# Sharing the first norm's rows between two engines and ending the last row block in two column halves

## The chip, the cores and the metric

The kernel runs on one core of a Trainium2 chip. A core has five engines, each with its own instruction queue: TensorE (PE, matrix products; its weight loads are listed as PEld), VectorE (DVE, elementwise and sums), ScalarE (ACT, functions of one operand), GpSimd (POOL) and SyncE (SP, which issues transfers). They wait for one another through semaphores. The metric is the time of one execution in microseconds (us). A lower time is better.

## The reference

One layer of a decoder on 1024 tokens of width 1024: a gated linear recurrence with 8 heads of 128, then a squared-ReLU MLP of width 4096, each behind an RMS norm, and a last RMS norm.

```python
def _rmsnorm(x, gain):
    xf = x.astype(jnp.float32)
    y = xf * lax.rsqrt(jnp.mean(xf * xf, axis=-1, keepdims=True) + NORM_EPS)
    return (y * gain.astype(jnp.float32)).astype(x.dtype)

def _hgrn2_mixer(h, w_in, lower_bound, out_norm, w_out):
    proj = h @ w_in
    q, f, i, g = jnp.split(proj, 4, axis=-1)
    ...
    o = _hgrn2_chunk_scan(heads(qf), heads(k), heads(i), heads(log_f))
    ...
    return o @ w_out

def _squared_relu_mlp(h, w1, w2):
    a = jax.nn.relu(h @ w1)
    return (a * a) @ w2

# DEPTH = 1
    x = x + _hgrn2_mixer(_rmsnorm(x, norm_mix), ...)
    x = x + _squared_relu_mlp(_rmsnorm(x, norm_mlp), mlp_w1, mlp_w2)
    return _rmsnorm(x, norm_final)
```

All inputs are float32.

## The kernel before

**Precision.** Each operand of a large product is split into a high part (`hi`, rounded by ACT) and the rest (`lo`, a subtraction on DVE). `split_mm` adds three matmuls: high by high, high by low, low by high (lines 212, 213, 214). The large products work on 2 by 2 blocks with sums and differences of blocks (names `s1` to `s4`, `t1` to `t4`), which saves one product in eight. `ht` is the split of such a sum of the normed input; `R` holds the unsplit values.

**The front.** `x` is loaded in eight row blocks of 128 tokens, `xs[0]` to `xs[7]`. For row blocks 0 to 3 a loop does, per block: the row's sum of squares on ACT (`stats_1`, line 293), the addition of EPS on DVE (line 297), the power -0.5 on POOL (line 298), the scaling of the whole block on DVE (`norm_scale`, line 186), four 128x128 transposes on PE (line 195) into four PSUM banks `first_banks`, and some transposes of `ident` that keep PE busy (`keep_warm`, line 123; `WARM_ROW` has their number per block). Then `transposes_1` moves each bank into the split operand `h0B` (ACT line 325, DVE line 326), with the gain.

**The hooks.** `plain_pair` computes the projections of head 0 with whole blocks: `w0` (a, c, b, d: q and f) and `w1` (i and g), first for the tokens of row blocks 0 to 3 (half 0), then for 4 to 7. Before each step of one weight block by one operand block (three matmuls) it calls `hook()`, which takes the next piece of work from a list: the remaining transposes of half 0, `value_1` (a copy of a bank to `R`), the sums of squares of row blocks 4 to 7, one addition and one power for the four of them (`rstd_second`), their scaling, then the transposes of half 1, one list entry in two. `ensure` splits the weights ahead of their use.

**The order on the engines.** PE's order is that of the code throughout. ACT, DVE and POOL follow the code in the very first part; from the end of half 0 until late in the output projection a scheduler orders them, and after that the code again. So a change of the code in the front also moves some instructions of the scan of head 0 (`lv` on PE, `q`, `qe`, `k`, `f` and `Ac` on DVE).

**The end.** In the last product of the MLP, job `d`, the four row blocks `pb` are done one after the other: 24 matmuls of 512 columns into the bank `m2X`, then `evac_2` adds the bank to `acc` (DVE, line 1071), and `rows_second_half` does the last norm: sum of squares of columns 512 to 1023 (ACT, line 1090), addition to the sum of the first half and power (POOL, lines 1092 and 1093), scaling (ACT line 1095, DVE line 1097) and two stores. Weights and operands of these products are float32 in the form `F32R`.

Of the kernel before, what the change touches and what calls it, by code (L numbers as in the profile page):

```python
# [42 lines left out]
LAST_SPACING = 1800.0  # L43
AHEAD = 6
WARM = 36
WARM_ROW = (6, 6, 6, 4)


@with_exitstack
def trunk(ctx: ExitStack, tc: tile.TileContext, x, gains, masks, gfin, w_in, w_out, w1, w2, out):  # L50
# [131 lines left out]
    def norm_scale(hn, src, r, on_act=False):  # L182
        if on_act:
            nc.scalar.activation(hn, src, AF.Copy, scale=r[:, 0:1])
        else:
            nc.vector.tensor_scalar(hn, src, r[:, 0:1], None, op0=ALU.mult)
# [65 lines left out]
    with tc.tile_pool(name="scan", bufs=1) as sp:  # L252
# [34 lines left out]
        def stats_1(tb):  # L287

            ss = ss4[:, tb - 4:tb - 3] if tb >= 4 else pool.tile([P, 1], F32, name=f"ss{tb}", tag="ss", bufs=8)
            if tb in (5, 7):  # L290
                nc.vector.tensor_tensor_reduce(junk[1], xs[tb], xs[tb], 1.0 / D, 0.0, ALU.mult, ALU.add, ss)
            else:
                nc.scalar.activation(junk[0], xs[tb], AF.Square, scale=D ** -0.5, accum_out=ss)
            return ss

        def rstd_1(r, ss):
            nc.vector.tensor_scalar(r, ss, EPS, None, op0=ALU.add)
            nc.gpsimd.tensor_tensor(r, r, neghalf[:, :r.shape[1]], ALU.pow)

        first_banks = [transpose_bank(0, 0, kb) for kb in range(4)]  # L300
        for tb in range(4):
            rs[tb] = pool.tile([P, 1], F32, name=f"rs{tb}", tag="rs1", bufs=8)
            rstd_1(rs[tb], stats_1(tb))
            norm_scale(xs[tb], xs[tb], rs[tb])
            for kb in range(4):
                transpose_rows(first_banks[kb], xs, kb, (tb,))
            keep_warm(WARM_ROW[tb])
# [43 lines left out]
        def pieces(f, *args):  # L351
            return lambda: [f(a) for a in args]

        def scale_1(tb):
            norm_scale(xs[tb], xs[tb], rs[tb])

        first = [lambda: (one[3](), value_1(0)), lambda: value_1(1), lambda: (one[4](), value_1(2)),
                 lambda: (one[5](), value_1(3)), one[6], one[7]]
        hooks += first

        def rstd_second():
            rstd_1(rs4, ss4)
            for i in range(4):
                rs[4 + i] = rs4[:, i:i + 1]

        hooks += [pieces(stats_1, 4, 5), pieces(stats_1, 6, 7), lambda: None, rstd_second, pieces(scale_1, 4, 5),
                  pieces(scale_1, 6, 7)] + [lambda: None] * 7
        for f in transposes_1(1):
            hooks += [f, lambda: None]

# [66 lines left out]
        def plain_pair(h, tl, j, half):  # L437

            steps = [(r, k) for r in range(2) for k in range(2)]
            if j == 0:  # L440
                steps.sort(key=lambda rk: rk[1])
            bank = {}
            for r, k in steps:
                if k == 0:
                    bank[r] = psum.tile([P, 512], F32, name=f"pp{h}{j}{half}{r}", tag="d")
                p_ = bank[r]
                m = "abcd"[2 * r + k]
                w = weight(2 * h + j, m)
                for kb in range(4):
                    hook()  # L450
                    t = hc[BLOCKS[half][k], kb]
                    c = slice(kb * P, (kb + 1) * P)
                    split_mm(p_, w[:, 0, c], w[:, 1, c], t[:, 0], t[:, 1], (k, kb) == (0, 0), (k, kb) == (1, 3))
                    i = index[2 * h + j, m]
                    if (j, half, m) == (0, 0, "a"):
                        ensure(2 + kb // 2)
                    elif kb == (0 if (j, half) == (0, 0) and m in "bc" else 2):
                        ensure(min(i + 3, 4 * PLAIN) if half == 0 else i + 4)
                    pump(650.0)
                if k == 0:  # L460
                    continue
                if (j, r) == (0, 0):
                    q_part(h, tl, 512 * half, p_)
                elif j == 0:
                    f_half(h, tl, half, p_, 1.0)
                    f_bound(h, tl["f"][:, HALF[half]])
                elif r == 0:
                    tiles(h, tl, "vT")
                    nc.scalar.activation(tl["vT"][:, HALF[half]], p_, AF.Copy)
                else:  # L470
                    g_half(h, tl, half, p_, 1.0)
# [590 lines left out]
    def fs(name):  # L1062
        return pool.tile([P, 1], F32, name=name, tag="fs", bufs=14)
# [16 lines left out]
    def rows_first_half(tb):  # L1080
# [4 lines left out]
        nc.vector.tensor_tensor(acc[tb][:, :512], acc[tb][:, :512], gf[:, :512], ALU.mult)  # L1085
        small[tb] = ss

    def rows_second_half(tb):
        ot, ss = out_tile(tb), fs(f"ft{tb}")
        nc.scalar.activation(ot[:, 512:], acc[tb][:, 512:], AF.Square, scale=D ** -0.5, accum_out=ss)  # L1090
        r = fs(f"fr{tb}")
        nc.gpsimd.tensor_tensor(r, ss, small[tb], ALU.add)
        nc.gpsimd.tensor_tensor(r, r, neghalf[:, :1], ALU.pow)
        rows = slice(tb * P, (tb + 1) * P)
        nc.scalar.activation(ot[:, :512], acc[tb][:, :512], AF.Copy, scale=r[:, 0:1])
        nc.scalar.dma_start(out[rows, :512], ot[:, :512])
        nc.vector.scalar_tensor_tensor(ot[:, 512:], acc[tb][:, 512:], r[:, 0:1], gf[:, 512:],
                                       op0=ALU.mult, op1=ALU.mult)
        nc.sync.dma_start(out[rows, 512:], ot[:, 512:])

    def product_2(k, pb, s, first, last_):
        hi, lo = sides[k]
        w = ws[k]
        for p in range(2):
            o, t = slice(512 * p, 512 * p + 512), slice(P * pb, P * pb + P)
            split_mm(banks[s, 0][pb], hi[:, p, t], lo[:, p, t], w[0][:, o], w[1][:, o], first and p == 0,
                     last_ and p == 1, skip_group_check=True)

    banks = {}
# [36 lines left out]
    for k, (which, u, v, s, m, n) in enumerate(steps):  # L1146
        first = m in ("a", "s1", "b")
        ending = which == 2 and u >= 4
        if first and v == 0:
            banks[s, u if which == 1 else 0] = [psum.tile([P, 512], F32, name=f"m{which}{s}{u}{p}", tag=BANK[s]) for p in range(2 * which)]  # L1150
        load_act(k + LOOK + 2)
        if which == 1:
            w = ws.pop(k)
            for p in range(2):
                for kb in range(4):
                    o = slice((4 * p + kb) * P, (4 * p + kb + 1) * P)
                    t = hc[n, kb]
                    if k == 1 or (k, p) == (0, 1) and kb > 1:
                        hook()
                    split_mm(banks[s, u][p], w[0][:, o], w[1][:, o], t[:, 0], t[:, 1], first and kb == 0, kb == 3,  # L1160
                             skip_group_check=True)
            if u + 1 < NU and m in ("s2", "s4"):
                load_w1(u + 1, "db" if m == "s4" else "ac" if u else "c")
            if u + 1 == NU and m in ("s2", "s4", "b"):
                for x in range(4):
                    load_w2({"s2": "a", "s4": "c", "b": "d"}[m], x)
            if k <= 8:
                for f in behind_0.get(k, ()):
                    f()
                continue  # L1170
            prep(k + LOOK)
            evac_1(u, m, e[u], banks[s, u])
            continue
        if (u, m) == (4, "a"):
            gf = dp.tile([P, D], F32, name="gf", tag="d8")
            nc.sync.dma_start(gf, bass.AP(tensor=gfin.tensor, offset=gfin.offset, ap=[[0, P], [1, D]]))
        if m == "a" and u < 4:
            load_acc(u)
        if m == "s1" and u < 4:
            load_w2("b", u)  # L1180
            load_acc(u + 4)
        if ending and m == "d":
            if v == 0:
                for pb in range(4):
                    for x in range(4):
                        product_2(k + x, pb, s, False, x == 3)
                    evac_2(m, pb, banks[s, 0][pb])
                    rows_second_half(pb)
            continue
        for pb in range(4):  # L1190
            product_2(k, pb, s, first and v == 0, v == 3)
        prep(k + LOOK)
        if m == "a":
            first_sums(raw2, u, slot(4 + v, [P, D], f"vs3{u}"))
        if ending and m == "b" and v == 3:
            prep(k + 3)
        if v == 3:
            for pb in range(4):
                evac_2(m, pb, banks[s, 0][pb])
        if ending and m == "b" and v < 2:  # L1200
            rows_out(4 + 2 * v)
            rows_out(5 + 2 * v)
        if ending and m == "b" and v == 3:
            prep(k + 4)
            for pb in range(4):
                rows_first_half(pb)
# [41 lines left out]
```

## Time and profile before

| what | value |
|---|---|
| median of 3 runs | 1148.96 us (1148.83 to 1149.08) |
| the profiled execution | 1148.8 us |
| span of its instructions | 1147.0 us |
| PE / DVE / ACT / POOL busy | 1133.5 / 797.2 / 583.7 / 37.9 us |
| first matmul of the projections | 13.26 us after the span's start |
| transposes of row blocks 4 to 7 begin / the next matmul | 29.31 / 31.38 us |
| last matmul starts / end of the span | 1139.79 / 1147.0 us |
| granted TensorE clock, mean | 0.999 |

The span runs from the first to the last instruction of the profiled execution; its own time holds 1.8 us more. A row of the timeline gives the start, the duration, the engine, the line, the operation, what it writes and reads, the size, and in brackets the idle time of the engine ahead of it and what ended it. Rows of one line that follow each other directly are merged (x4). A row of a single line's view gives the durations as least/median/most in ns.

### The profile page before, as it was taken

What the parts mean: (1) busy time and instruction counts of PE and PEld (TensorE: products, weight loads), DVE (VectorE), ACT (ScalarE), POOL (GpSimd) and SP (SyncE); (2) the same over time, 40 slices, a digit from 0 to 9 for tenths busy, and PEclk for the clock granted to TensorE, in tenths of its full rate; (3) what the DMA queues carried; (4) which work ended last, traced back from release to release, by engine and by line L of the source; (5) the groups of instructions that cost most, each with busy time, mean ns of one, the idle gap of its engine ahead of it and who ended that gap; (6) DMA issues with size and microseconds to landing.
All of it is one profiled execution on the core that took longest, in us unless ns stands there. A gap on an engine that the chain in (4) does not pass through costs nothing.

```text
span 1147.0 us, 17503 instructions
## 1 busy us (share of the span) xinstructions
PE 1133.5 (99%) x7082; PEld 936.8 (82%) x7082; DVE 797.2 (70%) x1145; ACT 583.7 (51%) x1014; POOL 37.9 (3%) x67
## 2 busy tenths in 40 slices
PE   9999999999999999999999999999999999999997
PEld 7778888787878788888888888888888888888886
DVE  6997878769687785446866654565488756677673
ACT  7656556374655573247654544454452443323552
POOL 1000000000000000010000000000000000000011
PEclk9999999999999999999999999999999999999999
DMA  6112211111111273021254524452797535322331
GB/s 262 37 38 68 61 40 56 56 38 57 56 50 63 68 264 130 26 85 74 76 200 184 187 86 149 183 197 82 269 367 295 195 136 207 124 92 94 127 129 73
DMA packets 42849, 142.84 MB, mean 125 GB/s; under 512 B 4880, under 2 KB 5008, under 8 KB 42768
## 3 DMA queue, kind: packets, MB, share of 16 engines
q1 hardware_dynamic: 41904, 140.53, 34.4%
q8 instruction: 55, 0.90, 0.3%
q10 hardware_dynamic: 864, 1.20, 0.3%
q14 instruction: 26, 0.21, 0.1%
HBM read 100.55 MB, written 41.16 MB: 124 GB/s over the span
## 4 chain that ended last, share of the span: by engine, by line
PE 86%; DVE 10%; ACT 1%; issue 1%; DMA 1%; POOL 0%; POOLq 0%; DVEq 0%; ACTq 0%
PE m2X L214 5%; PE m1X L213 5%; PE m2X L212 5%; PE m1X L212 5%; PE m1X L214 5%; PE m2X L213 5%; PE pX L212 3%; PE pX L214 3%; PE pX L213 3%; PE m1Y L212 3%; PE m1Y L213 3%; PE m2Y L214 3%; PE m2Y L212 3%; PE m1Y L214 3%; PE m2Y L213 3%; PE op L212 2%
## 5 line engine op out<-in xcount | busy, mean ns | idle before, releaser
L903 ACT ACTIVATE a<-ai 128x1024 fp32r<-128x1024 f32 x56 | 59.1, 1055 | 72.1 <-PE m2X L213 24.9
L904 DVE TENSOR_TENSOR a<-ai,a 128x1024 fp32r<-128x1024 f32 x56 | 68.3, 1220 | 11.5 <-ACT a L903 11.5
L994 ACT ACTIVATE e<-e 128x1024 f32<-128x1024 f32 x24 | 25.5, 1062 | 72.5 <-DVE e L1041 72.5
L212 PE MATMUL op<-wo,zh 128*128 128x512 f32 x128 | 51.1, 399 | 0.0
L214 PE MATMUL op<-wo,zh 128*128 128x512 f32 x128 | 50.0, 391 | 0.0
L213 PE MATMUL op<-wo,zh 128*128 128x512 f32 x128 | 49.9, 390 | 0.0
L1071 DVE TENSOR_TENSOR acc<-acc,m2X 128x512 f32<-128x512 f32 x32 | 21.1, 685 | 35.7 <-PE m2X L214 35.6
L145 DVE TENSOR_TENSOR xr<-xr,op 128x512 f32<-128x512 f32 x24 | 16.4, 687 | 38.1 <-PE op L214 38.1
L379 DVE TENSOR_TENSOR q<-q,f 128x512 f32<-128x512 f32 x56 | 38.5, 687 | 2.1 <-PE lv L627 2.1
L386 DVE TENSOR_TENSOR k<-k,f 128x512 f32<-128x512 f32 x56 | 38.3, 684 | 0.0
L991 ACT ACTIVATE e<-e 128x1024 f32<-128x1024 f32 x32 | 34.0, 1062 | 1.0
L604 ACT ACTIVATE AT<-Ac 32x256 f32<-32x256 f32 x32 | 13.3, 415 | 36.4 <-DVE Ac L600 36.1
L145 DVE TENSOR_TENSOR raw<-raw,raw 128x512 f32<-128x512 f32 x42 | 28.9, 688 | 0.8
L214 PEld LDWEIGHTS op<-wo,zh 128*128 128x128 f32 x128 | 24.0, 188 | 5.2
L212 PEld LDWEIGHTS op<-wo,zh 128*128 128x128 f32 x128 | 24.0, 188 | 4.8
L213 PEld LDWEIGHTS op<-wo,zh 128*128 128x128 f32 x128 | 24.1, 188 | 4.7
L696 ACT ACTIVATE z<-o,rs_z 128x128 f32<-128x128 f32 x64 | 17.4, 384 | 16.4 <-POOL rs_z L115 16.4
L1022 ACT ACTIVATE e<-m1X 128x512 f32<-128x512 f32 x30 | 16.9, 592 | 17.2 <-PE m1X L214 17.2
L684 PE MATMUL o<-v,AT 128*128 128x128 f32 x128 | 23.4, 275 | 0.0
L686 PE MATMUL o<-S,q 128*128 128x128 f32 x112 | 21.7, 275 | 0.0
L1071 DVE TENSOR_TENSOR acc<-acc,m2Y 128x512 f32<-128x512 f32 x16 | 10.8, 686 | 15.4 <-PE m2Y L214 13.8
L690 ACT ACTIVATE z<-o 128x128 f32<-128x128 f32 x64 | 16.8, 282 | 8.9 <-PE o L686 8.6
(1750 smaller groups left out, 3695.0 us busy)
## 6 DMA issues: line engine op xcount, KB each, us to landing
raw<-in_w_in SPq DMA_DIRECT2D x32, 512.0 KB, 3.7
ai<-adt SPq DMA_DIRECT2D x32, 512.0 KB, 4.6
adB<-e SPq DMA_DIRECT2D x24, 512.0 KB, 2.6
adt<-t SPq DMA_DIRECT2D x24, 512.0 KB, 4.8
ai<-adB SPq DMA_DIRECT2D x24, 512.0 KB, 4.5
x<-in_x SPq DMA_DIRECT2D x8, 512.0 KB, 7.4
iw<-in_w_out SPq DMA_DIRECT2D x16, 256.0 KB, 3.1
xr<-in_x SPq DMA_DIRECT2D x8, 512.0 KB, 5.5
```

Source lines behind the costliest of these rows:

```text
L145: nc.vector.tensor_tensor(out_, a, b, ALU.add)
L212: nc.tensor.matmul(ps, lhi, rhi, start=start, stop=False, **more)
L213: nc.tensor.matmul(ps, lhi, rlo, start=False, stop=False, **more)
L214: nc.tensor.matmul(ps, llo, rhi, start=False, stop=stop, **more)
L379: nc.vector.tensor_tensor(qo, qo, te.to_broadcast([P, n, m]), ALU.mult)
L386: nc.vector.tensor_tensor(ke, ke, to.to_broadcast([P, n, m]), ALU.mult)
L684: nc.tensor.matmul(ps[:, j, :], AT[:, c, :], v[:, c, :], start=True, stop=c == 0)
L903: nc.scalar.activation(hi, x, AF.Copy)
L904: nc.vector.tensor_tensor(lo, x, hi.bitcast(F32), ALU.subtract)
L991: nc.scalar.activation(t, t, AF.Square)
L994: nc.scalar.activation(t, t, AF.Relu, scale=sign)
L1071: nc.vector.tensor_tensor(t, t, ps, op)
```

## The change

It has five parts.

1. Row blocks 0 to 3: block 2 is scaled by ACT, not by DVE, and block 3's sum of squares is shared: columns 0 to 511 on ACT, 512 to 1023 on DVE (`tensor_tensor_reduce`). The addition takes both halves. The transposes of block 2 come after the instructions of block 3. `WARM_ROW` becomes 6, 12, 1, 4.
2. The first weight block `w0a` by half 0: per step, the two products with the high part of `h0B` come first, and the product with its low part one step later.
3. The hooks: one empty entry more ahead of `one[4]`, the sums of row blocks 4 to 7 in another order, row block 7 scaled by ACT, and a sigmoid of one column right behind the sums, so that ACT loads its table there. The transposes of half 1 come one hook later.
4. The weights are split one further ahead in places (`ensure(6)`, `i + 5`).
5. The last row block of job `d`: 18 matmuls into `m2X`, an addition, then six matmuls of 256 columns into `end0` and six into `end1`. Each is added and squared by itself; POOL adds the first half's sum early.

```diff
-WARM_ROW = (6, 6, 6, 4)
+WARM_ROW = (6, 12, 1, 4)
...
-        def rstd_1(r, ss):
-            nc.vector.tensor_scalar(r, ss, EPS, None, op0=ALU.add)
+        def rstd_1(r, ss, more=None):
+            if more is None:
+                nc.vector.tensor_scalar(r, ss, EPS, None, op0=ALU.add)
+            else:
+                nc.vector.tensor_scalar(r, ss, more, EPS, op0=ALU.add, op1=ALU.add)
             nc.gpsimd.tensor_tensor(r, r, neghalf[:, :r.shape[1]], ALU.pow)
...
-            rstd_1(rs[tb], stats_1(tb))
-            norm_scale(xs[tb], xs[tb], rs[tb])
+            if tb < 3:
+                rstd_1(rs[tb], stats_1(tb))
+            else:
+                two = pool.tile([P, 2], F32, name="ss3", tag="ss3")
+                half = slice(0, 512), slice(512, 1024)
+                nc.scalar.activation(junk[0][:, half[0]], xs[3][:, half[0]], AF.Square, scale=D ** -0.5,
+                                     accum_out=two[:, 0:1])
+                nc.vector.tensor_tensor_reduce(junk[1][:, half[1]], xs[3][:, half[1]], xs[3][:, half[1]], 1.0 / D, 0.0,
+                                               ALU.mult, ALU.add, two[:, 1:2])
+                norm_scale(xs[2], xs[2], rs[2], True)
+                rstd_1(rs[3], two[:, 0:1], two[:, 1:2])
+            if tb != 2:
+                norm_scale(xs[tb], xs[tb], rs[tb])
+            if tb == 3:
+                for kb in range(4):
+                    transpose_rows(first_banks[kb], xs, kb, (2,))
+                keep_warm(WARM_ROW[2])
+            if tb == 2:
+                continue
...
-            norm_scale(xs[tb], xs[tb], rs[tb])
+            norm_scale(xs[tb], xs[tb], rs[tb], tb == 7)
-        first = [lambda: (one[3](), value_1(0)), lambda: value_1(1), lambda: (one[4](), value_1(2)),
+        first = [lambda: (one[3](), value_1(0)), lambda: value_1(1), lambda: None, lambda: (one[4](), value_1(2)),
                  lambda: (one[5](), value_1(3)), one[6], one[7]]
...
-        hooks += [pieces(stats_1, 4, 5), pieces(stats_1, 6, 7), lambda: None, rstd_second, pieces(scale_1, 4, 5),
-                  pieces(scale_1, 6, 7)] + [lambda: None] * 7
+        def load_sigmoid():
+            nc.scalar.activation(two[:, 0:1], two[:, 0:1], AF.Sigmoid)
+        hooks += [pieces(stats_1, 4, 5), lambda: None, lambda: (stats_1(6), stats_1(7), rstd_second(), load_sigmoid()),
+                  pieces(scale_1, 7, 4, 5, 6)] + [lambda: None] * 9
...
-                    split_mm(p_, w[:, 0, c], w[:, 1, c], t[:, 0], t[:, 1], (k, kb) == (0, 0), (k, kb) == (1, 3))
+                    if (j, half, m) == (0, 0, "a"):
+                        nc.tensor.matmul(p_, w[:, 0, c], t[:, 0], start=kb == 0, stop=False)
+                        nc.tensor.matmul(p_, w[:, 1, c], t[:, 0], start=False, stop=False)
+                        for x in range(max(kb - 1, 0), kb if kb < 3 else 4):
+                            nc.tensor.matmul(p_, w[:, 0, x * P:(x + 1) * P], hc[BLOCKS[0][0], x][:, 1], start=False, stop=False)
+                    else:
+                        split_mm(p_, w[:, 0, c], w[:, 1, c], t[:, 0], t[:, 1], (k, kb) == (0, 0), (k, kb) == (1, 3))
...
+    def rows_last(tb, m, ends):
...
+        for c in range(2):
+            yield c
+            o = slice(512 + 256 * c, 768 + 256 * c)
+            t = acc[tb][:, o]
+            nc.vector.tensor_tensor(t, t, ends[c][:, :256], op)
+            nc.scalar.activation(ot[:, o], t, AF.Square, scale=D ** -0.5, accum_out=two[:, c:c + 1])
+            if c == 0:
+                nc.gpsimd.tensor_tensor(two[:, :1], two[:, :1], small[tb], ALU.add)
+        r = fs(f"fr{tb}")
+        nc.gpsimd.tensor_tensor(r, two[:, 1:2], two[:, :1], ALU.add)
+        nc.gpsimd.tensor_tensor(r, r, neghalf[:, :1], ALU.pow)
...
+                    if pb == 3:
+                        for x in range(3):
+                            product_2(k + x, pb, s, False, x == 2)
+                        evac_2(m, pb, banks[s, 0][pb])
+                        ends = [psum.tile([P, 512], F32, name=f"end{c}", tag="s") for c in range(2)]
+                        for c in rows_last(pb, m, ends):
+                            product_2(k + 3, pb, s, True, True, ends[c], c)
+                        continue
```

What remains of `rows_last` is as in `rows_second_half`.

DVE in the first four row blocks: `x_79` and `x_80` are row blocks 2 and 3, `rs` their factors, `ISA` the reduction and the reading of its sum. Before:

```order
L297 TENSOR_SCALAR rs_206<-ss_207 128x1
L186 TENSOR_SCALAR x_79<-x_79,rs_206 128x1024
L297 TENSOR_SCALAR rs_222<-ss_223 128x1
L186 TENSOR_SCALAR x_80<-x_80,rs_222 128x1024
L166 TENSOR_TENSOR w0a<-raw_139,w0a 128x128 x4
```

And now:

```order
L298 TENSOR_SCALAR rs_212<-ss_213 128x1
L313 ISA junk_169,ss_218<-x_80 128x512
L313 ISA ss_218 128x1
L300 TENSOR_SCALAR rs_217<-ss_218 128x1
L186 TENSOR_SCALAR x_80<-x_80,rs_217 128x1024
L166 TENSOR_TENSOR w0a<-raw_139,w0a 128x128 x4
```

The scaling of block 2 is gone from DVE, and the reduction stands directly behind the first addition.

DVE at the second four row blocks: `x_81` to `x_84` are row blocks 4 to 7, `lb` holds their four factors, `w1a` and `w1b` are splits of weights, `ht` a split of a sum. Before:

```order
L166 TENSOR_TENSOR w1a<-raw_147,w1a 128x512
L297 TENSOR_SCALAR lb<-lb 128x4
L186 TENSOR_SCALAR x_81<-x_81,lb 128x1024
L186 TENSOR_SCALAR x_82<-x_82,lb 128x1024
L186 TENSOR_SCALAR x_83<-x_83,lb 128x1024
L186 TENSOR_SCALAR x_84<-x_84,lb 128x1024
L415 SCALAR_TENSOR_TENSOR qd_368<-qd_368,qs,pp_256 128x16x32
L166 TENSOR_TENSOR w1b<-raw_148,w1b 128x512
```

And now:

```order
L105 TENSOR_TENSOR ht_562<-R_324,ht_562 128x512
L298 TENSOR_SCALAR lb<-lb 128x4
L166 TENSOR_TENSOR w1b<-raw_148,w1b 128x512
L186 TENSOR_SCALAR x_81<-x_81,lb 128x1024
L186 TENSOR_SCALAR x_82<-x_82,lb 128x1024
L186 TENSOR_SCALAR x_83<-x_83,lb 128x1024
L439 SCALAR_TENSOR_TENSOR qd_374<-qd_374,qs,pp_258 128x16x32
```

The split of `w1b` now stands between the addition and the scalings, of which one went to ACT.

ACT ahead of the scan of head 0, where a scheduler sets the order: `qd` is the sigmoid of q for half 1, read from PE's bank `pp`. Before:

```order
L165 ACTIVATE w2b<-raw_321 128x512
L104 ACTIVATE ht_550<-R_280 128x512
L104 ACTIVATE ht_553<-R_280 128x512
L414 ACTIVATE qd_368<-pp_577 128x16x32
L104 ACTIVATE ht_556<-R_312 128x512
```

And now:

```order
L165 ACTIVATE w2b<-raw_313 128x512
L104 ACTIVATE ht_770<-R_529 128x512
L104 ACTIVATE ht_553<-R_287 128x512
L438 ACTIVATE qd_374<-pp_580 128x16x32
L104 ACTIVATE ht_556<-R_287 128x512
L104 ACTIVATE ht_559<-R_324 128x512
```

Two of the eleven splits that DVE finishes there now have their copy behind `qd`, where one had; the seventh in DVE's order is the first of them.

More of the change, by code (lines that the diff above doesn't have):

```diff
@@ L452, in plain_pair @@
                     c = slice(kb * P, (kb + 1) * P)
-                    split_mm(p_, w[:, 0, c], w[:, 1, c], t[:, 0], t[:, 1], (k, kb) == (0, 0), (k, kb) == (1, 3))
+                    if (j, half, m) == (0, 0, "a"):
[5 more added lines that the diff above has]
+                        split_mm(p_, w[:, 0, c], w[:, 1, c], t[:, 0], t[:, 1], (k, kb) == (0, 0), (k, kb) == (1, 3))
                     i = index[2 * h + j, m]
+                    if (j, half, m, kb) == (0, 0, "b", 1):
+                        ensure(6)
                     if (j, half, m) == (0, 0, "a"):
@@ L457, in plain_pair @@
                     elif kb == (0 if (j, half) == (0, 0) and m in "bc" else 2):
-                        ensure(min(i + 3, 4 * PLAIN) if half == 0 else i + 4)
+                        ensure(min(i + 3, 4 * PLAIN) if half == 0 else i + 5)
                     pump(650.0)
@@ L1086, in rows_first_half @@
         small[tb] = ss
+    def rows_last(tb, m, ends):
+        half, dh, op = GOES[m]
+        ot = out_tile(tb)
+        two = pool.tile([P, 2], F32, name="ftwo", tag="ftwo")
+        for c in range(2):
[9 more added lines that the diff above has]
+        nc.gpsimd.tensor_tensor(r, r, neghalf[:, :1], ALU.pow)
+        rows = slice(tb * P, (tb + 1) * P)
+        nc.scalar.activation(ot[:, :512], acc[tb][:, :512], AF.Copy, scale=r[:, 0:1])
+        nc.scalar.dma_start(out[rows, :512], ot[:, :512])
+        nc.vector.scalar_tensor_tensor(ot[:, 512:], acc[tb][:, 512:], r[:, 0:1], gf[:, 512:],
+                                       op0=ALU.mult, op1=ALU.mult)
+        nc.sync.dma_start(out[rows, 512:], ot[:, 512:])
     def rows_second_half(tb):
@@ L1099, in rows_second_half, with product_2 @@
         nc.sync.dma_start(out[rows, 512:], ot[:, 512:])
-    def product_2(k, pb, s, first, last_):
+    def product_2(k, pb, s, first, last_, ps=None, half=None):
+        a, b = (0, 512) if half is None else (256 * half, 256 * half + 256)
+        ps = banks[s, 0][pb] if ps is None else ps[:, :b - a]
         hi, lo = sides[k]
@@ L1104, in product_2 @@
         for p in range(2):
-            o, t = slice(512 * p, 512 * p + 512), slice(P * pb, P * pb + P)
-            split_mm(banks[s, 0][pb], hi[:, p, t], lo[:, p, t], w[0][:, o], w[1][:, o], first and p == 0,
+            o, t = slice(512 * p + a, 512 * p + b), slice(P * pb, P * pb + P)
+            split_mm(ps, hi[:, p, t], lo[:, p, t], w[0][:, o], w[1][:, o], first and p == 0,
                      last_ and p == 1, skip_group_check=True)
```

## The prediction

> **What bounds the kernel now.** I read the busy line of the profile's page first, then the busy time by stages, and then the timeline at both ends of the span. Times are microseconds (us). The stages are cut at the first projection matmul, the end of the first norm's second half, the end of the first head's scan, and the last matmul.
>
> ```profile
> PE 1133.5 (99%) x7082; PEld 936.8 (82%) x7082; DVE 797.2 (70%) x1145; ACT 583.7 (51%) x1014; POOL 37.9 (3%) x67
> ...
> 0.00:13.26 13.26, 10.87 (x75) 9.68 (x75) 5.50 (x21) 7.64 (x16) 4.03 (x13) 1.00 0.87 340
> 13.26:31.38 18.12, 16.66 (x77) 12.41 (x78) 16.41 (x27) 15.87 (x27) 1.02 (x1) 1.00 0.46 166
> ...
> 92.00:1118.00 1026.00, 1023.16 (x6324) 847.25 (x6323) 705.96 (x981) 514.66 (x885) 28.12 (x41) 1.00 0.36 128
> ...
> 1140.20:1147.00 6.80, 0.00 (x0) 0.00 (x0) 1.44 (x2) 1.44 (x3) 0.74 (x2) 0.85 0.21 77
> ```
>
> The first two numbers of a stage are its length and TensorE's (PE's) busy time; PEld, DVE, ACT and POOL follow. In the 1026 us of the middle PE is busy but for 2.84 us, and the change leaves the order of work there alone. What it can win stands at the ends: 1.46 us without PE work before 31.38, warm-up work on ident ahead of 13.26, and 6.80 us after the last matmul. So I cost the front, what of it lasts to the steady part, and the tail. The sum is made against the profiled execution: its own time is 1148.8, span 1147.0 and 1.8 around it. The median of the runs is 0.16 above it, and I add that at the end. 0.2% is 2.3 us, about what a measurement of this kernel can tell from no change.
>
> **The first four rows.** Per row block, the row's mean square goes through DVE (rs), POOL (the power) and DVE again (scale), then PE transposes it:
>
> ```profile
> 8.87 1.06 ACT L293 ACTIVATE junk<-x 128x1024 f32<-128x1024 f32 x1
> 9.03 0.15 DVE L297 TENSOR_SCALAR rs<-ss 128x1 f32<-128x1 f32 x1
> 9.26 0.55 POOL L298 TENSOR_TENSOR rs<-rs,neghalf 128x1 f32<-128x1 f32 x1 [0.93 <-DVE rs L297]
> 9.84 0.75 DVE L186 TENSOR_SCALAR x<-x,rs 128x1024 f32<-128x1024 f32 x1 [0.66 <-POOL rs L298]
> 11.32 0.77 DVE L186 TENSOR_SCALAR x<-x,rs 128x1024 f32<-128x1024 f32 x1 [0.66 <-POOL rs L298]
> 12.15 0.66 PE L195 MATMUL tr<-ident,x 128*128 128x128 f32 x4 [0.19 <-DVE x L186]
> 12.51 2.42 ACT L325 ACTIVATE h0B<-tr,gn 128x512 fp32r<-128x512 f32 x4 [1.51 <-PE tr L195]
> ...
> 23.70 1.22 DVE L291 CUSTOM_DVE_ANT_0 junk<-x 128x1024 f32<-128x1024 f32 x1
> ...
> L184 ACT ACTIVATE hm<-xr,rs_n x2: 1138/1138/1139, 492.7 to 498.1; 128x1024 f32<-128x1024 f32 x2
> ```
>
> One row block takes 11.32 - 9.84 = 1.48, and the transposes of row block 3 wait for its scale (12.15); from 12.51 ACT, DVE and PE run on. Now DVE squares half of row 3 while POOL computes the power of row 2, and ACT scales row 2. With nothing in the way: ACT's scale starts at 9.85, takes 1.14 (L184), row 2 is transposed at 11.05; row 3's rs follows half of 1.22, its power would end by 10.8, and its scale starts there instead of at 11.32. Row 3's transposes would stand near 11.65, a gain of 0.5.
>
> But something is in the way. These three rows, from the second norm, show a POOL instruction alone, and one that met a DVE instruction with two tensors read from SBUF:
>
> ```profile
> 487.50 0.23 POOL L114 TENSOR_SCALAR rs_n<-ss 128x1 f32<-128x1 f32 x1 [25.62 <-ACT hm L179]
> ...
> 509.45 1.23 DVE L145 TENSOR_TENSOR uc<-uc,ud 128x1024 f32<-128x1024 f32 x1
> 509.55 1.20 POOL L114 TENSOR_SCALAR rs_n<-ss 128x1 f32<-128x1 f32 x1 [4.91 <-ACT junk L179]
> ```
>
> The same instruction takes 0.23 alone and 1.20 beside the DVE add: it ends at 510.75, 0.07 after the add. The Trainium skill, "SBUF — State Buffer", section "SBUF: two separate sides", states it as a rule: a GpSimd instruction that reads SBUF and a DVE instruction with two SBUF inputs exclude one another, and the later one waits for the whole of the earlier one. By that rule the trace agrees, 1.20 against 0.23.
>
> Before, DVE waited while POOL worked (0.66 idle ahead of each scale). Now the reduction of row 3, which reads x3 twice, follows rs directly, near 9.12, while POOL starts only 0.23 after rs, at 9.26. I take half of 1.22 and some start, 0.65 to 0.69; the power of row 2 is held to 9.8 and ends near 10.3 in place of 9.81. ACT then scales from 10.30, row 2 is transposed from 11.50 to 11.94, one warm-up matmul, and row 3 at 12.05 (its own scale starts near 10.92, as POOL is free again; ready 0.83 later, by 11.75). The gain at 12.15 is 0.1, not 0.5.
>
> **The second four rows.**
>
> ```profile
> 27.20 0.17 DVE L297 TENSOR_SCALAR lb<-lb 128x4 f32<-128x4 f32 x1
> 27.44 1.02 POOL L298 TENSOR_TENSOR lb<-lb,neghalf 128x4 f32<-128x4 f32 x1 [15.10 <-DVE lb L297]
> 28.50 2.74 DVE L186 TENSOR_SCALAR x<-x,lb 128x1024 f32<-128x1024 f32 x4 [1.14 <-POOL lb L298]
> 31.38 0.48 PE L212 MATMUL pp<-h0B,w1a 128*128 128x512 f32 x1
> 31.82 0.69 DVE L166 TENSOR_TENSOR w1b<-raw,w1b 128x512 fp32r<-128x512 f32 x1
> 32.16 0.39 PE L212 MATMUL pp<-h0B,w1b 128*128 128x512 f32 x1
> 32.39 0.39 PE L213 MATMUL pp<-h0B,w1b 128*128 128x512 f32 x1
> ```
>
> Between 12.51 and 27.20 DVE and ACT are full, and the same instructions stand ahead of rs in a changed order. The new order of the first matmuls (both products with the high part first) and the transposes that come one hook later only fill PE's waits, and PE has to wait at the scales in any case. So rs comes at 27.1, 0.1 earlier. Behind it DVE now has the split of w1b, 0.69, with two SBUF inputs, where it used to wait for POOL: the power, due at 27.34, is held to 27.8 and ends near 28.8. The scales start at 28.83, 0.33 later than before. There are three on DVE, 0.66 apart, and one on ACT (1.14, done by 30.0). The last is the third on DVE, at 30.15; ready 0.81 later, and PE has its matmul at 31.15 instead of 31.38. PE meanwhile has done three matmuls of w1a that stood behind the wait before (31.38 to 32.16). Compared at the second matmul of w1b, behind the slow first one (0.32): 32.39 before, 31.15 + 0.32 = 31.47 now. PE is ahead by 0.92. Without either collision it would be 1.8.
>
> The early table load, a dummy sigmoid of 128x1, moves 1.3 us of ACT from behind the row sums to a place where ACT next has to wait for the power anyhow; I cost it at nothing. Its cover is that wait. If the cover were gone, DVE's rs would slip, since the split ht in front of it needs ACT's half; by the order the two come within 0.1 of each other.
>
> **What of that lasts.** Up to 85 us DVE is nearly always busy, and PE's scan matmuls come as DVE lets them:
>
> ```profile
> 47.39 2.49 DVE L105 TENSOR_TENSOR ht<-R,ht 128x512 fp32r<-128x512 f32 x4
> 50.49 4.30 DVE L105 TENSOR_TENSOR ht<-R,ht 128x512 fp32r<-128x512 f32 x7 [0.62 <-ACT ht L104]
> 52.03 0.60 ACT L414 ACTIVATE qd<-pp 128x512 f32<-128x512 f32 x1 [1.04 <-PE pp L214]
> 54.72 0.74 DVE L415 SCALAR_TENSOR_TENSOR qd<-qd,qs,pp 128x512 f32<-128x512 f32 x1
> 56.57 1.23 DVE L520 TENSOR_TENSOR q<-qd,f 128x1024 f32<-128x1024 f32 x1 [0.51 <-ACT f L424]
> ...
> 68.22 0.69 DVE L573 TENSOR_TENSOR qe<-q,f 128x512 f32<-128x512 f32 x1
> ...
> 69.06 0.89 PE L579 MATMUL lv<-qe,k 128*32 128x48 f32 x64
> ```
>
> PE's lv matmuls at 69.06 need qe, started 0.84 ahead of them. To gain there, DVE must be earlier too. Of its eleven splits ht, the seventh now needs a copy that ACT does behind qd, and qd waits for PE: 52.03 - 0.92 = 51.11, the copy 0.49 later, ready at 52.25. DVE gets there by about 51.4 and waits (it would have to be 0.8 later still for this not to decide). Then five splits of 0.61 (4.30 over 7), qd and the split of w2a (54.72 to 56.57 less 0.51 idle, 1.34) bring q to 56.6, as before. On the way to qe the new order has two splits fewer and one sum more, -0.61. So qe starts at 67.6, PE's matmuls come at 68.45, and 0.6 of the 0.92 is left. The following scan steps keep that distance by the same order. Front: **-0.6**. Its ends: nothing at all, and 1.5 (no collision; the same count with PE 1.8 ahead then finds qe at 66.7 and PE 1.5 ahead).
>
> **The tail.**
>
> ```profile
> 1138.66 0.39 PE L212 MATMUL m2X<-vd7sh,a 128*128 128x512 f32 x1
> ...
> 1139.79 0.39 PE L214 MATMUL m2X<-vd7sh,a 128*128 128x512 f32 x1
> 1140.22 0.69 DVE L1071 TENSOR_TENSOR acc<-acc,m2X 128x512 f32<-128x512 f32 x1 [2.31 <-PE m2X L214]
> 1140.94 0.63 ACT L1090 ACTIVATE ot<-acc 128x512 f32<-128x512 f32 x1 [3.05 <-DVE acc L1071]
> ...
> 90.51 1.72 PE L665 MATMUL kv<-v,kt 128*128 128x128 f32 x14
> ...
> L671 DVE SCALAR_TENSOR_TENSOR S<-S,tot,kv x48: 346/348/349, 92.5 to 453.5; 128x128 f32<-128x128 f32 x48
> ...
> L690 ACT ACTIVATE z<-o x64: 262/278/325, 97.3 to 459.4; 128x128 f32<-128x128 f32 x64
> ```
>
> After the last matmul comes a chain: add (0.69), square with its sum (0.63), POOL's add and power, scale, store. Only the add and the square become narrower on that path; the first half's add, square and POOL add run beside the second half's matmuls. Nothing else of the chain is removed. No row has 256 columns. The add: 0.69 at 512, 0.35 for a like instruction at 128, so 0.43; -0.26. The square: 0.63 at 512, 0.28 at 128, so 0.40; -0.24. PE now does twelve matmuls of 256 columns for six of 512 at (1139.79 - 1138.66) / 5 = 0.226. At 128 columns fourteen take 1.72, 0.111 each after the first 0.275, weight loads included. The bounds per matmul are 0.111 and 0.226. I take 0.12: the stream of 256 columns is half of 0.226, and the row at 128 shows that a weight load fits into 0.111. Twelve then take 1.44 for 1.36; with the shorter drain of a narrow matmul the second half's add starts 0.11 later. Tail: -0.26 - 0.24 + 0.11 = **-0.4**; its ends are -0.5 and, at 0.226 per matmul, +0.8.
>
> Sum: 1148.8 - 0.6 - 0.4 = 1147.8, and on the scale of the median **1147.9**.
>
> **The rivals.** *No collision.* If DVE's instructions don't hold POOL in these two places, the front gives 1.5 and the time is 1147.0. For it: both are short instructions, and which one comes first hangs on 0.1 us. Against it: 509.55.
>
> *DVE gives all of it back.* If DVE reaches q 0.6 later than I count, the lv matmuls of 69.06 don't move, and the tail alone is left: 1148.5. For it: DVE was just in time there before.
>
> *The narrow matmuls cost as much as the wide ones*, and the kernel gets slower. The place is the last twelve matmuls; at 0.226 each the tail is +0.8 and the time 1149.1. It decides from 0.215 on: 12 x 0.215 is 1.2 over the 1.36 of before, which eats the other 1.1. For it: twice the weight loads, PEld 82% busy. Against it: 0.111 at 128 columns. The Trainium skill, "TensorE: Matmul & The Clock Gate", section "LDWEIGHTS (loading the stationary operand)", says that a load's time goes by the weights' columns, so halving the moving columns halves none of it; by its 128/1.2, 107 ns, behind each 109 ns of stream and not hidden, an estimate gives 0.216 per pair and a time of 1149.0. The trace's 0.111 for load and matmul together speaks against it.
>
> *More than I see.* The first matmuls' new order lets other waits go as well, and the time falls under 1146.6.
>
> **How the numbers follow.** My forecast 0.55; no collision 0.2; all given back 0.11; narrow matmuls 0.06; more than I see 0.08. The range is 1146.8 to 1148.8: it takes in no collision and the bound of everything given back, and leaves out the last two. Faster by over 0.2%: 0.18, the last case and part of the second, whose 1147.0 is 0.4 short of that bound. Slower by over 0.2%: 0.04, narrow matmuls far over 0.226 or a longer wait at the scales. Within: 0.78.
>
> **What would show it.** In the new profile the power of row 2 should last about 1.0 instead of 0.55, the power of the second four rows about 1.5 instead of 1.02, and PE's first matmul of w1b should stand near 31.15. The lv matmuls of qe should start near 68.45, and PE's last matmul should end within 0.15 of 1140.2 less 0.6. From there to the end should be 6.3 instead of 6.8. If both powers have their old length, the first rival holds; if the twelve matmuls take over 2 us, the third.

## The result, and the profile after

The changed kernel takes 1165.72 us (1165.65 to 1165.79), the kernel before 1149.02 in the same runs. The ratio is 1.0145, with a 95% interval from 1.0133 to 1.0158: it is slower by 16.7 us. I had said 1147.9. The profiled execution took 1165.79, its span is 1164.0.

The page's busy line, which stands against PE's 1133.5 of before:

```profile
PE 1152.1 (99%) x7089; PEld 938.6 (81%) x7089; DVE 798.3 (69%) x1147; ACT 584.8 (50%) x1019; POOL 38.8 (3%) x68
```

PE is busy 18.6 us longer, for the same products; the other engines are within 1.1 us of what they were. The busy time by stages (columns as before) shows that this is not at the ends. The middle 1026 us are again full for PE at a clock of 1.00, but hold 6248 matmul records where there were 6324:

```profile
92.00:1118.00 1026.00, 1023.20 (x6248) 833.20 (x6248) 693.34 (x967) 504.27 (x872) 26.66 (x38) 1.00 0.35 124
```

So in the same time and at the same clock fewer matmuls fit, and on average each is a little slower. The timeline of a place in the MLP where PE waits for nothing:

```profile
1128.16 0.40 PE L212 MATMUL m2Z<-vb6sh,a 128*128 128x512 f32 x1
...
1130.96 0.40 PE L212 MATMUL m2Z<-vb7sh,a 128*128 128x512 f32 x1
```

Thirteen starts lie between and including these rows, twelve steps in 2.80: 0.2333 each. Before, the same kind of matmul came every 0.226 to 0.227 (1138.66 to 1139.79 in the prediction). Not all of them are slower. Two groups of the costliest, by line, before and then after (mean ns of one behind the comma):

```profile
L212 PE MATMUL op<-wo,zh 128*128 128x512 f32 x128 | 51.1, 399 | 0.0
...
L684 PE MATMUL o<-v,AT 128*128 128x128 f32 x128 | 23.4, 275 | 0.0
```

```profile
L212 PE MATMUL op<-wo,zh 128*128 128x512 f32 x128 | 51.7, 404 | 0.0
...
L717 PE MATMUL o<-v,AT 128*128 128x128 f32 x128 | 23.4, 275 | 0.0
```

The matmuls of 512 columns in the output projection lost 5 ns of the mean; the ones of 128 columns in the scan lost nothing. The width need not be the reason: by the addresses that follow, the two operands of the second group have moved alike.

The steps that I had worked out came nearly as I had said. This is the timeline of the changed kernel at the places of the prediction:

```profile
6.62 0.55 POOL L301 TENSOR_TENSOR rs<-rs,neghalf 128x1 f32<-128x1 f32 x1 [5.30 <-DVE rs L298]
...
9.42 0.68 DVE L313 CUSTOM_DVE_ANT_0 junk<-x 128x512 f32<-128x512 f32 x1
9.58 1.48 POOL L301 TENSOR_TENSOR rs<-rs,neghalf 128x1 f32<-128x1 f32 x2 [0.93 <-DVE rs L298]
10.54 1.15 ACT L184 ACTIVATE x<-x,rs 128x1024 f32<-128x1024 f32 x1 [0.97 <-POOL rs L301]
12.35 0.60 PE L195 MATMUL tr<-ident,x 128*128 128x128 f32 x4
...
27.36 0.68 DVE L166 TENSOR_TENSOR w1b<-raw,w1b 128x512 fp32r<-128x512 f32 x1
27.54 1.39 POOL L301 TENSOR_TENSOR lb<-lb,neghalf 128x4 f32<-128x4 f32 x1 [15.42 <-DVE lb L298]
31.29 0.48 PE L212 MATMUL pp<-h0B,w1b 128*128 128x512 f32 x1
...
68.47 0.89 PE L612 MATMUL lv<-qe,k 128*32 128x48 f32 x64 [0.24 <-DVE qe L606]
```

Both powers were held by a DVE instruction that reads two SBUF tensors. The first one held the power of row 2 until ACT's scale could start at 10.54 (I said 10.3); the second one lasted 1.39 (I said about 1.5). The lv matmuls stand at 68.47 (I said 68.45; this trace starts its first power at 6.62, the one of before at 6.29, and what that does to the comparison stands further below). The end of the span:

```profile
1156.06 0.28 PE L212 MATMUL end<-vd7sh,a 128*128 128x256 f32 x1
...
1157.35 0.28 PE L214 MATMUL end<-vd7sh,a 128*128 128x256 f32 x1
1157.67 0.42 DVE L1130 TENSOR_TENSOR acc<-acc,end 128x256 f32<-128x256 f32 x1 [0.19 <-PE end L214]
1158.12 0.42 ACT L1131 ACTIVATE ot<-acc 128x256 f32<-128x256 f32 x1
```

Twelve matmuls of 256 columns take eleven steps in 1.29, 0.117 each. From the first of the last product's matmuls to the end of the span there are now 1164.0 - 1156.06 = 7.94; before it was 1147.0 - 1138.66 = 8.34. That is the -0.4 of the prediction. If the front gave its -0.6 as well, some 17.7 us were lost in between, in work that the diff does not mention.

**What the diff moves without naming it.** The order of the instructions is the same in that stretch, on PE, DVE, ACT and POOL. What differs is where tiles lie. The change allocates two new tiles called `two` (tags `ss3` and `ftwo`), 8 bytes per partition each. By the compiled program's addresses each takes 32 bytes of pool `keep`: what is allocated in that pool behind the first lies 32 bytes further, behind both 64, and the pools laid out after it (`scan`, `mlp`) lie 64 bytes further. Pool `right` (`dp`), which is laid out from the other end and holds one operand of most large products, stays. So I took from the compiled program of each kernel the start address of the moving and of the stationary operand of each matmul of 512 columns, and counted their difference (moving minus stationary) modulo 256 bytes:

| kernel | 0 | 32 | 128 | 192 | 224 | not 0 |
|---|---|---|---|---|---|---|
| before | 4440 | | | | | 0 |
| after | 1536 | 456 | | 264 | 2178 | 2898 |
| e1_padded | 4434 | | | | | 0 |
| e2_shift | 1536 | 456 | | 264 | 2184 | 2904 |
| e6_pad128 | 1800 | | 2634 | | | 2634 |
| e8_noedge | 2976 | 1464 | | | | 1464 |

Set beside the trace of after, matmul by matmul from 60 us on and without the steps of over 0.3 us, which hold waits, the mean step is 0.2333 at 32, 0.2334 at 192, 0.2332 at 224, and 0.2282 (median 0.227) at 0; before, where all are at 0, it is 0.2273. The theory: a matmul of 512 columns costs some 0.006 more where its two operands start at different places modulo 256 bytes (first I took it for 128, which these two kernels cannot tell apart). The rival: the changed order, or the longer program, slows PE.

### The profile page after: what moved, and what is told of

It reads as the page before. It is cut to its first block, busy times and chain, and to the rows that moved or that the text cites. A ratio compares the mean times of both kernels' runs of the same rounds, so it can differ in the third digit from the quotient of the medians.

```text
span 1164.0 us, 17525 instructions
## 1 busy us (share of the span) xinstructions
PE 1152.1 (99%) x7089; PEld 938.6 (81%) x7089; DVE 798.3 (69%) x1147; ACT 584.8 (50%) x1019; POOL 38.8 (3%) x68
## 4 chain that ended last, share of the span: by engine, by line
PE 87%; DVE 9%; ACT 2%; issue 1%; DMA 1%; POOL 0%; POOLq 0%; DVEq 0%; ACTq 0%
PE m2X L212 5%; PE m2X L213 5%; PE m2X L214 5%; PE m1X L212 5%; PE m1X L214 5%; PE m1X L213 5%; PE pX L212 4%; PE pX L214 3%; PE pX L213 3%; PE m2Y L212 3%; PE m2Y L214 3%; PE m2Y L213 3%; PE m1Y L212 3%; PE m1Y L213 3%; PE m1Y L214 3%; PE op L212 2%
```

## The experiments

**e1_padded: the change with its two tiles made larger.** Nothing else differs from the changed kernel.

```diff
-                two = pool.tile([P, 2], F32, name="ss3", tag="ss3")
+                two = pool.tile([P, 64], F32, name="ss3", tag="ss3")
...
-        two = pool.tile([P, 2], F32, name="ftwo", tag="ftwo")
+        two = pool.tile([P, 64], F32, name="ftwo", tag="ftwo")
```

> The changed kernel with its two new tiles (8 bytes per partition each) made 256 bytes each; every engine has the same instructions in the same order. By the compiled addresses all 4434 matmuls of 512 columns then read their moving and their stationary operand at starts that are equal modulo 128 bytes, as before the change; in the changed kernel 2898 of them do not. Address theory: the spacing goes back to 0.227 and the time to the blind sum, 1147.9 (1147.0 to 1148.8). Rival, that the changed order or the changed program slows the matmuls: it stays at 1165 to 1166.

Measured: 1147.97 (1147.72 to 1148.26) beside 1148.89 for the kernel before; ratio 0.9992 (0.9983 to 1.0001). The whole 17.75 are gone. Its middle stage and a stretch in the MLP:

```profile
92.00:1118.00 1026.00, 1022.86 (x6321) 846.87 (x6320) 705.81 (x980) 514.70 (x886) 28.19 (x41) 1.00 0.36 127
```

```profile
1127.83 0.39 PE L213 MATMUL m2X<-vd7sl,a 128*128 128x512 f32 x1
...
1129.87 0.39 PE L213 MATMUL m2X<-vd4sl,a 128*128 128x512 f32 x1
```

Nine steps in 2.04, 0.2267, and 6321 records in the stage. The rival falls: the order and the length of the program are those of the slow kernel.

**e2_shift: the kernel before with the two small tiles alone.**

```diff
             rs[tb] = pool.tile([P, 1], F32, name=f"rs{tb}", tag="rs1", bufs=8)
+            if tb == 3:
+                pool.tile([P, 2], F32, name="ss3", tag="ss3")
...
+        if tb == 3:
+            pool.tile([P, 2], F32, name="ftwo", tag="ftwo")
         r = fs(f"fr{tb}")
```

> The kernel before with the two 8-byte tiles declared at the same places and never used: no instruction is added, removed or moved, only addresses behind them shift by 32 and 64 bytes; 2904 of the 4440 matmuls of 512 columns get starts that differ modulo 128. Address theory: 1149.0 + about 2800 x 0.0065 = 1167 (1165 to 1169), with the spacing at 0.233 where the starts differ. Rival, the order of work: 1149.0, as nothing of it changes.

Measured: 1166.65, ratio 1.0153 (1.0140 to 1.0167). No instruction differs from the kernel before, and 17.76 us are lost: 0.0061 for each of the 2904 matmuls. The middle stage and the group of above:

```profile
92.00:1118.00 1026.00, 1023.58 (x6254) 833.57 (x6253) 693.29 (x969) 504.27 (x872) 26.54 (x38) 1.00 0.34 124
```

```profile
L212 PE MATMUL op<-wo,zh 128*128 128x512 f32 x128 | 51.7, 404 | 0.0
```

**m_stream: the cost by itself.** A chain of matmuls, in stages that differ in the operands' starts alone, all of them with weights that alternate between two places 512 bytes apart where nothing else is said; it leaves out the whole layer.

> Only a copy of x to the output and a row of 23 stages of 48 matmuls, one after the other, with no other engine at work beside them; it leaves out the whole of the reference. Stages: the moving tile's start shifted against the weights by 0, 4, 16, 32, 48, 64, 96, 128, 192, 256 and 512 bytes; the weights' start shifted by 32, 64 and 128; both by 16, 32 and 64; weights that alternate between shifts 0 and 32 with a moving tile that fits each matmul's own weights, or the next one's; one weight tile over and over at 0 and 32; 256 columns at 0 and 32. Address theory: 0.2267 per matmul for differences of 0, 128, 256 and 512 and wherever both are shifted alike, 0.233 for 32, 64 and 96 and probably for the rest. If the load of the next weights is what meets the stream, the stage that fits the next one's is the fast one of that pair; if it is the matmul's own weights, the other. Rival, that it needs other engines' traffic on SBUF: 0.2267 in all stages.

Some of its stages in the trace, by line; the weights start at 0, and the moving operand at 0 (pa), 64 (pf), 96 (pg), 128 (ph), 256 (pj), both at 32 (pp); pv and pw are 256 columns at 0 and 32:

```profile
L95 PE MATMUL pg<-mv,wt 128*128 128x512 f32 x48 | 11.4, 395 | 0.0
...
L99 PE MATMUL ph<-mv,wt 128*128 128x512 f32 x48 | 11.4, 395 | 0.0
...
L91 PE MATMUL pf<-mv,wt 128*128 128x512 f32 x48 | 11.2, 392 | 0.0
...
L107 PE MATMUL pj<-mv,wt 128*128 128x512 f32 x48 | 11.1, 389 | 0.0
...
L131 PE MATMUL pp<-mv,wt 128*128 128x512 f32 x48 | 11.1, 389 | 0.0
...
L71 PE MATMUL pa<-mv,wt 128*128 128x512 f32 x48 | 11.0, 389 | 0.0
L155 PE MATMUL pv<-mv,wt 128*128 128x256 f32 x48 | 5.9, 283 | 0.0
L159 PE MATMUL pw<-mv,wt 128*128 128x256 f32 x48 | 5.8, 280 | 0.0
```

The mean step from start to start, in ns:

| moving start against the weights' | 0 | 4 | 16 | 32 | 48 | 64 | 96 | 128 | 192 | 256 | 512 |
|---|---|---|---|---|---|---|---|---|---|---|---|
| step | 226.7 | 236.6 | 231.7 | 233.0 | 233.2 | 229.1 | 233.6 | 233.4 | 233.2 | 227.1 | 226.7 |

The weights shifted by 32, 64, 128: 233.2, 233.4, 232.5. Both shifted by 32 and by 64: 226.7 and 227.2; both by 16: 231.0. One weight tile over and over: 226.9 at 0 and 233.4 at 32. So no other engine is needed. For shifts by 32 and 64 the difference decides and not the place; both shifted by 16 is an exception that I can't explain. And I was wrong on the period: 128 bytes cost as much as 32. Padding to 256 in e1 had been lucky; 128 would have read as an alignment just as well. Neither of the two pure forms of "own weights or next weights" holds: a moving tile that fits its own weights but not the next gave 232.1, one that fits the next alone 230.5.

**e6_pad128: the test of the period in the kernel.** As e1, with `[P, 32]` in place of `[P, 64]`.

> The changed kernel with its two new tiles made 128 bytes each. Differences of the starts are then 0 modulo 128 for all 4434 matmuls of 512 columns, but 128 modulo 256 for 2634 of them. Period of 256 bytes, as the row of stages alone showed: 1148.0 + about 2500 x 0.0065 = 1164 (1163 to 1165). Period of 128, which is all that the kernels before and after could tell: 1148.0.

Measured: 1162.70 (1162.60 to 1162.73), ratio 1.0120 (1.0105 to 1.0136), 14.7 us above e1, 0.0056 for each of the 2634 matmuls. So 128 bytes is not the period in the kernel either; with the fast stages at 256 and 512 it is 256 bytes.

**e3_front and e4_tail: the change in two parts**, with the starts kept equal. e3 leaves out the branch `if pb == 3` of the last job, e4 is the kernel before with that branch, `rows_last` and the new `product_2` alone; the tile that is left in each is `[P, 64]`.

> The change without its last part (the last block's end is as before), with the one new tile made 256 bytes, so that all 4440 matmuls of 512 columns read at starts equal modulo 256 bytes. My sum gives the front -0.6: about 1148.3 beside 1148.9 before. Rival, the front gives nothing that lasts and the whole gain of the padded change is its tail: 1148.9.

> The kernel before with the last part of the change alone, its new tile made 256 bytes. My sum gives the tail -0.4: about 1148.5 beside 1148.9 before; the last twelve matmuls, 256 columns wide, 0.12 us each. Rival, the narrow matmuls cost as much as the wide ones: 1149.7.

Measured: e3 1148.34 and e4 1148.62, beside 1148.89; ratios 0.9995 (0.9986 to 1.0004) and 0.9998 (0.9989 to 1.0006). So -0.55 and -0.27, where I had -0.6 and -0.4; by the times alone, neither is told from no change.

**e5_row3: without the first collision.** e1 with row block 3's sum of squares whole on ACT:

```diff
-                two = pool.tile([P, 64], F32, name="ss3", tag="ss3")
-                half = slice(0, 512), slice(512, 1024)
-                nc.scalar.activation(junk[0][:, half[0]], ...
-                nc.vector.tensor_tensor_reduce(junk[1][:, half[1]], ...
+                two = stats_1(3)
                 norm_scale(xs[2], xs[2], rs[2], True)
-                rstd_1(rs[3], two[:, 0:1], two[:, 1:2])
+                rstd_1(rs[3], two)
```

> The padded change with the sum of squares of row block 3 whole on ACT again, as before the change (DVE has no half of it; row block 2 is still scaled on ACT). DVE then reads no two SBUF tensors while POOL computes the power of row block 2. Theory of the collision: that power, together with row block 3's 1.48 us in two, falls to 0.55 each; row block 2's scale starts about 0.35 earlier, row block 3's transposes stand 0.3 to 0.4 earlier against the first power, though ACT has more to do; the time is 1147.6 to 1148.0, the same as the padded change or up to 0.35 less. Rival, the half on DVE is what gains: row block 3's transposes come 0.4 later and the time is 1148.3.

Measured: 1147.32 (1147.02 to 1147.51), ratio 0.9986 (0.9977 to 0.9995): 0.65 under e1, more than I expected. The two were not run side by side, but each beside a kernel before at 1148.89, and the slowest run of e5 is faster than the fastest of e1 (1147.72). Its timeline:

```profile
6.49 0.55 POOL L301 TENSOR_TENSOR rs<-rs,neghalf 128x1 f32<-128x1 f32 x1 [5.16 <-DVE rs L298]
...
9.45 0.55 POOL L301 TENSOR_TENSOR rs<-rs,neghalf 128x1 f32<-128x1 f32 x1 [0.93 <-DVE rs L298]
...
10.03 1.15 ACT L184 ACTIVATE x<-x,rs 128x1024 f32<-128x1024 f32 x1
10.18 0.55 POOL L301 TENSOR_TENSOR rs<-rs,neghalf 128x1 f32<-128x1 f32 x1 [0.19 <-DVE rs L298]
...
11.84 0.60 PE L195 MATMUL tr<-ident,x 128*128 128x128 f32 x4
...
30.77 0.48 PE L212 MATMUL pp<-h0B,w1b 128*128 128x512 f32 x1
...
67.91 0.89 PE L607 MATMUL lv<-qe,k 128*32 128x48 f32 x64 [0.22 <-DVE qe L601]
```

Each power is back at 0.55. Counted from the first power (6.49; 6.62 in the changed kernel), row block 3's transposes stand at 5.35 instead of 5.73, and the lv matmuls at 61.42 instead of 61.85. DVE's half of row 3 cost more than it brought: ACT has the whole sum done by 9.92, and DVE's share only held the power of row 2. These 0.43 are not all of the 0.65 yet; the rest comes near 330 us (see the front, below).

**e7_order: without the second collision too.** e5 with the scales of the second four rows issued right behind their power, ahead of the split of w1b:

```diff
-        hooks += [..., lambda: (stats_1(6), stats_1(7), rstd_second(), load_sigmoid()),
-                  pieces(scale_1, 7, 4, 5, 6)] + [lambda: None] * 9
+        hooks += [..., lambda: (stats_1(6), stats_1(7), rstd_second(), load_sigmoid(),
+                                pieces(scale_1, 7, 4, 5, 6)())] + [lambda: None] * 10
```

> The kernel of e5 with one more change: the scales of the second four rows are issued in the step of their power, so on VectorE they stand ahead of the split of w1b, which now follows them; nothing else moves. No two-tensor read of VectorE then meets a power of the first norm. Theory of the collision: the power falls from 1.39 to 1.02, the scales start about 0.37 earlier after rs, w1b's split is done about as late as PE needs it, and the time is 0 to 0.2 under e5's 1147.3; the rival of the prediction, no collision, said 1147.0. Other outcome: PE now waits for the split of w1b, its second matmul with w1b stands later than in e5, and the time is 1147.6 or more.

Measured: 1147.29 (1147.06 to 1147.66), ratio 0.9986 (0.9977 to 0.9995), the same as e5.

```profile
6.32 0.55 POOL L301 TENSOR_TENSOR rs<-rs,neghalf 128x1 f32<-128x1 f32 x1 [4.99 <-DVE rs L298]
...
26.86 1.02 POOL L301 TENSOR_TENSOR lb<-lb,neghalf 128x4 f32<-128x4 f32 x1 [15.21 <-DVE lb L298]
...
30.24 0.48 PE L212 MATMUL pp<-h0B,w1b 128*128 128x512 f32 x1
...
67.77 0.89 PE L607 MATMUL lv<-qe,k 128*32 128x48 f32 x64 [0.23 <-DVE qe L601]
```

The power is 1.02 again, and from the first power PE has w1b at 23.92 instead of e5's 24.28. But the lv matmuls stand at 61.45 against 61.42: what PE won at 30 us is gone by 68. As far as these runs can tell, the second collision cost nothing that lasts.

**m_stream2: where the loss ends.** The same chain with other starts, columns and types.

> A second row of 23 stages of 48 matmuls, alone on the core, which leaves out the whole of the reference but for a copy of x to the output. Moving start against weights by 0, 160, 224, 288 and 1024 bytes: with a period of 256 bytes 0.2267 at 0 and 1024, 0.231 to 0.236 at the others. Both by 128: 0.2267. Weights alternating between 0 and 128, with the moving tile that fits the own or the next weights, and only one of the two alternating: if a matmul's own pair alone counted, the stage that fits its own would be fast; if the load of the next weights alone counted, the one that fits the next; in the first row both were slow (0.232 and 0.2305), so I expect 0.229 to 0.234 for all four. 384, 320 and 256 columns at 0 and 32: if the loss belongs to each pair of a load and a stream, it is 0.006 again as long as the stream is the longer of the two, and nothing at 256, as in the first row (0.120 and 0.118). Weights of 64 columns: the load is shorter, and the loss is half. bfloat16: another period or none; nothing in this case shows it.

Steps in ns: differences of 160, 224 and 288 give 234.1, 233.3 and 233.3, 1024 gives 227.5, both at 128 226.8. Weights between 0 and 128 with a moving tile that fits its own: 228.6, the next: 230.0; only the moving one alternating 231.7, only the weights 234.8. With 384 columns it is 173.8 at 0 and 173.3 at 32, with 320 columns 146.5 and 146.6, with 256 119.8 and 117.9. With weights of 64 columns 230.1 and 231.2, so slower at 0 as well, which I had not expected. In bfloat16 the median is 216 at every start. My guess that 384 columns would lose 6 ns fell. Of the types and widths tried (those under 512 columns at 0 and 32 alone), the loss belongs to float32r at the full 512 columns.

**e8_noedge: the same effect in the kernel before.** Pool `right` holds a tile that nothing reads or writes. I left it out:

```diff
-        dp.tile([P, 8], F32, name="edge")
```

> The kernel before without its tile edge (L758, 8 float32 per partition, 32 bytes, which no instruction reads or writes); no instruction changes. The tiles of pool right that follow move by 32 bytes; by the compiled addresses 1464 of the 4440 matmuls of 512 columns then read at starts that differ by 32 modulo 256 bytes, the other 2976 by 0. Address theory, with 0.0061 a matmul from the run of the shift alone (17.8 over 2904): 1148.9 + 8.9 = 1157.8 (1157 to 1159). Rival, that an unused tile does nothing: 1148.9.

Measured: 1157.12 (1156.92 to 1157.21) beside 1148.94, ratio 1.0071 (1.0054 to 1.0088): 8.2 us for 1464 matmuls, 0.0056 each. By the addresses these are 504 of the projections, 384 of the output projection and 576 of the MLP's first products. An unused 32 bytes kept their two sides in step, and the change undid that from the other side.

## Why the prediction was wrong

- **The failed step** is the one that has no term in my sum: the middle of 1026 us, set aside with "the change leaves the order of work there alone". The order did stay. But I took the cost of one matmul as fixed when the order is fixed, and the two 8-byte tiles as free. They cost 1165.72 - 1147.97 = 17.75 us. None of my rivals had a mechanism in that stretch, so the range could not hold the time either.
- **The sum of the named parts** came out: 1147.9 foretold, 1147.97 with the tiles padded. Against the kernel before alone this is weak, since the interval of that ratio (0.9983 to 1.0001) takes in no change; the traces bear it out: from the first power of the first norm to the end of the span, e1 takes 1146.5 - 6.67, before 1147.0 - 6.29, which is 0.9 less where the parts add up to 1.0.
- **The front**, -0.6: -0.55 by the times of e3. The traces start their first power between 6.29 and 6.70, also where the front is that of before (6.70 in e2). Counted from that power the traces agree: the lv matmuls stand at 62.77 before, 62.74 in e2, 62.72 in e4. The changed kernel has them at 61.85 (e1 61.85, e3 61.81), 0.9 earlier and not 0.6; that 68.47 met my 68.45 is luck, as this trace's later first power hides 0.33 of the gain. Nor do the scan steps keep the distance, as I had it. Matmul by matmul, and from the first power, e1 and e3 are 0.97 and 0.95 ahead of before at 306 us, and 0.56 and 0.58 in the MLP. So the size was right and the way to it was not: 0.3 more was won, and 0.4 is given back near 330 us. A part of that is a wait of PE for DVE, which e1 has (first row) and e5 does not (second row):

```profile
330.99 0.46 PE L660 MATMUL lv<-q,k 128*32 128x32 f32 x32 [0.36 <-DVE k L410]
```

```profile
330.01 0.46 PE L655 MATMUL lv<-q,k 128*32 128x32 f32 x32
```

In the MLP e5 is 1.40 ahead of before. Why DVE is late there in e1 stays open. The collision was real, as priced from 509.55. The Trainium skill, "SBUF — State Buffer", section "SBUF: two separate sides", has it as an exclusive lock for a whole instruction; the runs agree (0.55 each without a two-tensor read of DVE beside them, 1.48 for the two with one). The wait for ht behind qd was there too: DVE's seventh split starts at 52.31, after 0.81 of waiting for ACT's copy.
- **"No collision"**, 1147.0: e7 has none and takes 1147.29, with the lv matmuls 1.3 earlier from the first power (I said 1.5). It gets there without DVE's half of row 3, so it is not quite the kernel of that rival, but the price was near. The first collision made nearly all of it.
- **The tail**, -0.4: -0.27 by the times of e4, -0.40 by the trace of after and -0.32 by that of e1 (8.02 from the first of the twelve matmuls to the end); the spans are given to 0.1, so these two agree. The twelve at 0.12 took 0.117 to 0.120, the narrow add and square 0.42 each against 0.43 and 0.40 (a straight line between its two rows would have put the add at 0.46). The rival's estimate from the Trainium skill, "TensorE: Matmul & The Clock Gate", section "LDWEIGHTS (loading the stationary operand)", 0.216 for a load and a matmul of 256 columns, did not come.
- **The early table load** at nothing: rs of the second four rows did not slip (27.29, 20.67 after the first power; 27.20, 20.91 after it before).

What stays open is why. The loss hangs on the starts of the moving operand and of the weights, it needs no other engine, and it depends mostly on their difference. Stages that fit a matmul's own weights alone, or the next one's alone, were both slow; that a read of one operand meets a read of the other is a guess, and no run shows it. Nor did I try strides, or other types than the two.

## What to carry to other kernels

Where PE is full and streams 512 columns of float32r, compare the compiled start addresses of both operands modulo 256 bytes before and after any change that adds, removes or resizes a tile, however small, in a pool ahead of the operands; keep the difference as it was, which padding new tiles to 256 bytes per partition did here. When a kernel gets slower everywhere by about one per cent at an unchanged order and clock, look at the step between back-to-back matmuls of one shape first. And a share of work given to an idle engine is not free if it holds a third engine's short instruction: the version without DVE's half (e5, 1147.32) beats the kernel before (1148.89) and, by the medians, the padded change (1147.97).

## What the runs showed of the hardware

- The step of 512-column float32r matmuls is 0.2267 to 0.2275 (median 0.227) when moving and stationary start are equal modulo 256 bytes, also if both are shifted alike by 32, 64 or 128, but not if both are by 16 (0.2310); it is 0.229 to 0.237 otherwise. The clock was 1.00 in these stages, and PE alone at work.
- At 384 and 320 columns a difference of 32 changed the step by 0.5 ns at most; at 256 columns it was 2 ns shorter. In bfloat16 at 512 columns the median was 216 ns at 0, 32, 64, 128 and 256.
- Weights of 64 columns did not make the step shorter than weights of 128: 0.2301 against 0.2267.
